# Differential values of both head pairs in one product with 512 moving columns, heads started one chunk earlier in the chunk list, background step every 16 matmuls

## The chip, the cores and the metric

The kernel runs on one core of a Trainium2 chip. The metric is the device time of one execution in microseconds (us), less is better. The engines named below are TensorE (PE, with its weight loads as PEld), VectorE (DVE), ScalarE (ACT), GpSimd (POOL) and SyncE (SP). "Product" means a matrix product of the kernel, made of many PE matmuls.

## The reference, cut to what matters

One layer over 512 prompt tokens and 64 sample tokens, model width 1024, all in float32: a half-step SwiGLU feed-forward, a mixer with one combined projection, and a second half-step SwiGLU feed-forward, each between two RMSNorms.

```
x = x + 0.5 * rms(swiglu(rms(x)))
h = rms(x);  p = h @ w_in          # columns: retention q|k|v|gate, differential q1q2|k1k2|v
q_d = rope(q_d.reshape(b, l, 4, 2, 64)); k_d = rope(...)
v_d = v_d.reshape(b, l, 4, 128)    # 4 heads of 128 columns; an output of its own (new_v)
a = softmax(s1) - lam * softmax(s2);  diff = rms(a @ v_d)
x = x + rms(concat(ret, diff) @ w_out)
x = x + 0.5 * rms(swiglu(rms(x)))
```

The changed product is `v_d`: 576 tokens x 1024 by 1024 x 512 columns, that is two pairs of heads with 256 columns each.

## The kernel before, in words

Tokens are cut into two halves of 256 and 320 (the second holds 256 prompt and 64 sample tokens). Every product is made with both operands split into a high and a low fp32r part (`whi`/`wlo` of a weight tile, `hhi`/`hlo` of the input), so each 128-deep step takes three matmuls. A weight tile is 128 x 512; SP loads it (256 KB, `raw`), ACT casts it to `whi` (L126) and DVE subtracts to `wlo` (L127). Twelve such pairs are held.

The mixer runs from 404.3 us to about 724 us of the span. Its projection is cut into 14 chunks of 256 columns in the order `IN_ORDER`: vd0, qd0, kd0, qd1, kd1, vd1, kr0, qr0, vr0, kr1, qr1, vr1, gr0, gr1 (d differential, r retention, 0 and 1 the head pair), then four chunks of the output projection. Each chunk is done for half 0 and then half 1. The first `FIRST` = 3 chunks form a group: all three for half 0, then all three for half 1, so that the boundary from the first feed-forward can finish half 1 meanwhile. In a q, k or gate chunk the weights are stationary and 256 or 320 token columns move (L434 to L436). In a v chunk (`natural()`, L806 to L808) 128 tokens are stationary and the chunk's 256 weight columns move, 48 matmuls a half; the 64 sample tokens of half 1 are a third block with 16 matmuls (`sample()`).

PSUM has two double buffers `pm` (a product's two banks) and four single banks `ps`. A q or k product in a `pm` buffer is read by three DVE instructions of `rotate()`: a shuffle (L757), and two multiplications (L758, L759). L757 and L758 read the PSUM buffer, so it is free when L758 is done. The next product but one needs that buffer.

Attention of a pair of heads is "background": `heads()` is a generator (score products `sc`, row maxima on DVE, exponentials on ACT, transposes `tp`, products with the values `av`, and for the differential pairs a final norm `finish()` with the sums `oss`). It is added to `self.bg` after a chunk given by `plan` (pair d0 after kd0, d1 after vd1, r0 after vr0, r1 after vr1). `pump()` counts the matmuls of the running product and makes one step of it for every `PUMP` = 18. Emission order is what the engines get, apart from the static order that the Tile scheduler derives from it. Before the first output chunk (`chunks[14]`) what is left in the background is drained.

Of the kernel before, what the change touches and what calls it, by code (L numbers as in the profile page):

```python
# [37 lines left out]
W_BUFS = 12  # L38
RK = 2
RAW_BUFS, RAW2_BUFS = 3, 5  # L40
FIRST, LAST_FFN, LAST_MIX = 3, 4, 3
PUMP = 18
B_NOW = {2: 2, 4: 0}
QK_BUFS = 5
WARM = 11
V_PS = (("vd", 0),)
N2 = 7


# [4 lines left out]
NB = (((0, 0, 128), (1, 128, 128)), ((2, 0, 128), (3, 128, 128), (4, 256, 64)))  # L54


class Weights:
# [6 lines left out]
        self.nc, self.raw, self.pool, self.raw2 = nc, raw_pool, w_pool, None  # L64
        self.parts, self.src, self.loaded, self.done = [], [], [], []

    def add(self, ap, nk, both=False):

        first = len(self.parts)
        for k in range(0, nk, RK):  # L70
            self.parts.append(("plain", len(self.src)))
            self.src.append((ap[:, k:k + RK, :], both and len(self.src) % 3 > 0))
        return list(range(first, len(self.parts)))

    def unit(self, ap):
# [72 lines left out]


class Layer:  # L150
    IN_ORDER = [("vd", 0), ("qd", 0), ("kd", 0), ("qd", 1), ("kd", 1), ("vd", 1), ("kr", 0), ("qr", 0), ("vr", 0),
                ("kr", 1), ("qr", 1), ("vr", 1), ("gr", 0), ("gr", 1)]

    def __init__(self, nc, tc, ctx, io):
# [573 lines left out]
    def mixer(self, h, post_g, next_g):  # L728
        nc, tc, io = self.nc, self.tc, self.io
# [5 lines left out]
        with ExitStack() as ctx:  # L735
            pool = lambda name, bufs=1: ctx.enter_context(tc.tile_pool(name=name, bufs=bufs))
            rt, qkp, vp, pp, atp, cp, op = (
                pool("rt"), pool("qk", QK_BUFS), pool("vp"), pool("pp", 3), pool("atp", 1), pool("cp"), pool("op"))
            rope = {}
            q, k, v, gate = {}, {}, {}, {}  # L740
# [21 lines left out]
            def project(name, c, half):  # L762
                n = HN[half]
                kind = name[-1]
                if name[0] == "v":
                    return natural(name, c, half)
                if name[0] in "qk" and (kind, half) not in rope:
                    tables(kind, half)
                ps = self.product(self.w_in[name, c], half, self.h_parts(h, half))[0][1]
                if name[0] == "g":  # L770
                    g = gf = qk_tile(half, "gate")
                    nc.vector.tensor_tensor(gf, ps, r[half].unsqueeze(1).broadcast_to([P, 2, n]), ALU.mult)
                    nc.scalar.activation(gf, gf, AF.Silu)
                    gate[c, half] = g
                    return
                a, b = rotate(ps, kind, half)
                t = qk_tile(half, name)
                nc.vector.tensor_tensor(t, a, b, ALU.add)
                for kk in range(2):
                    (q if name[0] == "q" else k)[kind, 2 * c + kk, half] = t[:, kk, :]  # L780
                if name == "kd":
                    nc.gpsimd.dma_start(out=io["k_out"][:, 2 * c:2 * c + 2, HOFF[half]:HOFF[half] + n], in_=t)

            def natural(name, c, half):

                kind = name[-1]
                pieces = self.w_in[name, c]
                hp = self.h_parts(h, half)
                for first in range(0, len(NB[half]), 2):
                    blocks = NB[half][first:first + 2]  # L790
                    if (name, c) in V_PS:
                        ps = self.ps1("psv").rearrange("p (b d) -> p b d", b=2)
                    else:
                        ps = self.pm.tile([P, 2, 512], F32, tag="pm", name="pmv")
# [17 lines left out]
                    t = vp.tile([P, 2, 256], F32, tag="v2", name=name, bufs=4)  # L812
                    for bi, (b, off, m) in enumerate(blocks):
                        nc.scalar.activation(t[:m, bi, :], ps[:m, bi, :256], AF.Copy,
                                             scale=self.rnat[half][:m, first + bi:first + bi + 1])
                        for kk in range(2):
                            v[kind, 2 * c + kk, b] = t[:m, bi, kk * P:(kk + 1) * P]
                        if name == "vd":
                            nc.gpsimd.dma_start(out=io["v_out"][b * P:b * P + m, c * 256:(c + 1) * 256],
                                                in_=t[:m, bi, :])  # L820

            def sample(name, c, pieces, ps):
# [12 lines left out]
                for kk in range(2):  # L835
                    v[name[-1], 2 * c + kk, 4] = t[:TS, kk * P:(kk + 1) * P]
                if name == "vd":
                    nc.gpsimd.dma_start(out=io["v_out"][TP:, c * 256:(c + 1) * 256], in_=t[:TS, :])

            def o_tiles(shared):  # L840
                if shared:
# [296 lines left out]
            def heads(kind, pair):  # L1138
                o = held[kind, pair] = o_tiles((kind, pair) == ("r", 0))
                make = diff_items if kind == "d" else ret_items  # L1140
                yield from pipeline(make(2 * pair, o) + make(2 * pair + 1, o))
                if kind == "d":
                    yield from finish(kind, pair)

            held = {}
            plan = {("kd", 0): [lambda: heads("d", 0)], ("vd", 1): [lambda: heads("d", 1)],
                    ("vr", 0): [lambda: heads("r", 0)], ("vr", 1): [lambda: heads("r", 1)]}

            def proj(name, c):
# [12 lines left out]
            chunks[14] = (chunks[14][0], lambda half, fn=chunks[14][1]: (self.drain(), fn(half)))  # L1162
            self.run(self.halves(chunks, FIRST, LAST_MIX))
        return after

    def build(self):
        nc, io = self.nc, self.io
        self.w_in = {}
        self.plan = [self.ffn_weights(0)]
        for i, key in enumerate(self.IN_ORDER):  # L1170
            self.w_in[key] = self.w.add(io["win"][i], KT)
# [30 lines left out]
        h = []  # L1202
# [14 lines left out]
        h = self.ffn(0, h, 0, 1, 2)  # L1217
# [82 lines left out]
def arrays_of(inp):  # L1300

    c = np.ascontiguousarray
    a = {}
# [19 lines left out]
    perm = ret_perm()  # L1323
    perm2 = np.concatenate([perm, 128 + perm])
    win = []
    for name, ch in Layer.IN_ORDER:
# [43 lines left out]
```

## Time and profile before

| what | value |
|---|---|
| median of 3 runs | 1130.77 us (1130.28 to 1130.91) |
| profiled execution | 1130.78 us, span 1129.0 us, 1.8 us lie around the span |
| PE busy over the span | 1115.6 us (99%) |
| DVE busy | 840.9 us (74%) |
| ACT busy | 579.5 us (51%) |
| POOL busy | 39.0 us (3%) |
| granted TensorE clock, mean | 0.996 |

The busy times overlap. A row of the timeline has a start, a duration, the engine, the line, what is written and read with shapes, a count where like instructions follow each other, and in brackets the idle time of that engine just before it and what ended it. Successive PE matmuls overlap, so a matmul costs the distance of two starts, not its duration.

### The profile page before, as it was taken

Reading aid. Unit: us, or ns where it says so; the run is one execution under the profiler, and the core shown is the slowest. Engines: PE = TensorE matmul, PEld = TensorE weight load, DVE = VectorE, ACT = ScalarE, POOL = GpSimd, SP = SyncE. Lnnn points to the kernel's source line nnn. Section 1 sums busy time; section 2 is a strip of 40 time slices with the busy share of each in tenths; the row PEclk is TensorE's granted clock in tenths of the full one; section 3 lists DMA queues with packets and bytes.
Section 4 is the critical chain, followed back from the end, with each engine's and each line's share of the span. In section 5 each row is a group of like instructions: output and inputs, shape, how many; then the busy total and the mean of one; then the engine's idle time right before and its main releaser. Section 6 shows DMA issues by size and latency. Waiting matters only on the chain.

```text
span 1129.0 us, 21258 instructions
## 1 busy us (share of the span) xinstructions
PE 1115.6 (99%) x8308; PEld 1096.2 (97%) x8308; DVE 840.9 (74%) x1646; ACT 579.5 (51%) x1112; POOL 39.0 (3%) x76
## 2 busy tenths in 40 slices
PE   8999999999999999999999999999999999999997
PEld 8999999999999999898999999999999999999997
DVE  7898865876587499869775585899886578658745
ACT  7666632562365465555442555666555156325543
POOL 0000000000000020010001010100000000000000
PEclk9999999999999999999999999999999999999999
DMA  8303431351236133332313221640334124313602
GB/s 278 90 29 113 125 101 38 106 139 55 76 88 212 39 115 106 97 110 60 98 58 89 83 69 39 198 120 16 92 115 135 38 85 124 101 38 105 203 2 84
DMA packets 57317, 109.22 MB, mean 97 GB/s; under 512 B 7008, under 2 KB 10336, under 8 KB 57216
## 3 DMA queue, kind: packets, MB, share of 16 engines
q1 hardware_dynamic: 51856, 91.97, 27.7%
q0 software_dynamic: 4352, 14.68, 3.9%
q8 instruction: 65, 1.06, 0.4%
q10 hardware_dynamic: 1008, 1.20, 0.3%
q14 instruction: 36, 0.29, 0.1%
HBM read 100.23 MB, written 7.60 MB: 96 GB/s over the span
## 4 chain that ended last, share of the span: by engine, by line
PE 90%; DVE 5%; DMA 2%; ACT 2%; issue 1%; DVEq 0%; SPq 0%; ACTq 0%
PE pm L435 11%; PE pm L434 11%; PE pm L436 11%; PE A L529 7%; PE A L530 7%; PE A L531 7%; PE C L531 3%; PE C L530 3%; PE C L529 3%; PE pb L434 2%; PE pa L434 2%; PE pb L436 2%; PE pa L435 2%; PE pa L436 2%; PE pb L435 2%; PE B L529 2%
## 5 line engine op out<-in xcount | busy, mean ns | idle before, releaser
L126 ACT CAST whi<-raw 128x512 fp32r<-128x512 f32 x336 | 206.7, 619 | 258.6 <-PE pm L435 98.4
L127 DVE TENSOR_TENSOR wlo<-raw,whi 128x512 fp32r<-128x512 f32 x336 | 229.6, 688 | 84.9 <-ACT whi L126 80.0
L434 PE MATMUL pm<-hhi,whi 128*128 128x320 f32 (+1 forms) x496 | 151.6, 306 | 1.9 <-ACT hhi L254 1.9
L435 PE MATMUL pm<-hlo,whi 128*128 128x320 f32 (+1 forms) x496 | 148.5, 299 | 0.3 <-DVE hlo L255 0.3
L436 PE MATMUL pm<-hhi,wlo 128*128 128x320 f32 (+1 forms) x496 | 148.1, 299 | 0.0
L434 PE MATMUL pm<-a,whi 128*128 128x320 f32 (+1 forms) x452 | 134.0, 297 | 0.4 <-ACT y L661 0.4
L435 PE MATMUL pm<-a,whi 128*128 128x320 f32 (+1 forms) x452 | 134.0, 297 | 0.4 <-DVE a L187 0.4
L436 PE MATMUL pm<-a,wlo 128*128 128x320 f32 (+1 forms) x452 | 134.1, 297 | 0.0
L529 PE MATMUL A<-tb,whi 128*128 128x288 f32 x432 | 128.0, 296 | 0.0
L530 PE MATMUL A<-tb,whi 128*128 128x288 f32 x432 | 127.5, 295 | 0.0
L531 PE MATMUL A<-tb,wlo 128*128 128x288 f32 x432 | 127.0, 294 | 0.0
L126 ACT CAST whi<-wsum 128x512 fp32r<-128x512 f32 x108 | 67.1, 621 | 68.8 <-PE A L530 17.0
L434 PEld LDWEIGHTS pm<-hhi,whi 128*128 128x128 f32 x496 | 94.8, 191 | 4.3 <-ACT hhi L254 2.1
L435 PEld LDWEIGHTS pm<-hlo,whi 128*128 128x128 f32 x496 | 94.8, 191 | 1.1 <-DVE hlo L255 0.5
L436 PEld LDWEIGHTS pm<-hhi,wlo 128*128 128x128 f32 x496 | 94.7, 191 | 0.1
L127 DVE TENSOR_TENSOR wlo<-wsum,whi 128x512 fp32r<-128x512 f32 x108 | 74.6, 691 | 21.2 <-ACT whi L126 18.9
L434 PEld LDWEIGHTS pm<-a,whi 128*128 128x128 f32 x452 | 85.8, 190 | 0.7 <-ACT y L661 0.6
L435 PEld LDWEIGHTS pm<-a,whi 128*128 128x128 f32 x452 | 85.8, 190 | 0.6 <-DVE a L187 0.6
L436 PEld LDWEIGHTS pm<-a,wlo 128*128 128x128 f32 x452 | 85.8, 190 | 0.0
L531 PEld LDWEIGHTS A<-tb,wlo 128*128 128x128 f32 x432 | 81.3, 188 | 0.0
L529 PEld LDWEIGHTS A<-tb,whi 128*128 128x128 f32 x432 | 80.9, 187 | 0.2
L530 PEld LDWEIGHTS A<-tb,whi 128*128 128x128 f32 x432 | 81.1, 188 | 0.0
(348 smaller groups left out, 2904.0 us busy)
## 6 DMA issues: line engine op xcount, KB each, us to landing
raw<-in_w0gs SPq DMA_DIRECT2D x72, 256.0 KB, 2.7
raw<-in_w1gs SPq DMA_DIRECT2D x72, 256.0 KB, 2.7
raw<-in_win SPq DMA_DIRECT2D x56, 256.0 KB, 3.1
raw<-in_w0d SPq DMA_DIRECT2D x44, 256.0 KB, 2.8
raw<-in_w1d SPq DMA_DIRECT2D x44, 256.0 KB, 2.8
raw<-in_w0gu SPq DMA_DIRECT2D x16, 256.0 KB, 5.8
raw<-in_wout SPq DMA_DIRECT2D x16, 256.0 KB, 3.0
raw<-in_w1gu SPq DMA_DIRECT2D x16, 256.0 KB, 3.4
```

What stands on the lines that cost most here:

```text
L126: nc.scalar.copy(hi, raw)
L127: nc.vector.tensor_tensor(lo, raw, hi.bitcast(F32), ALU.subtract)
L434: nc.tensor.matmul(outs[c], lhsT=hi[:, k, cs], rhs=rh, start=kt == 0, stop=False)
L435: nc.tensor.matmul(outs[c], lhsT=hi[:, k, cs], rhs=rl, start=False, stop=False)
L436: nc.tensor.matmul(outs[c], lhsT=lo[:, k, cs], rhs=rh, start=False, stop=kt == len(kts) - 1)
L529: nc.tensor.matmul(out, lhsT=hi[:, k, :], rhs=rh, start=first and k == 0, stop=False, skip_group_check=True)
L530: nc.tensor.matmul(out, lhsT=hi[:, k, :], rhs=rl, start=False, stop=False, skip_group_check=True)
L531: nc.tensor.matmul(out, lhsT=lo[:, k, :], rhs=rh, start=False, stop=last and k == 3, skip_group_check=True)
```

## The change

The two vd chunks become one, first in the list, with weights `wvd` whose 128 x 512 tiles each hold one 128-deep step of all 512 columns (`rk=1`) instead of two steps of 256. `wide()` makes the product with 512 moving columns into a `pm` buffer, one bank for each block of 128 tokens; `wide_sample()` does the sample tokens into one `ps` bank. The evictions then go to four tiles as before. There are 13 instead of 14 input chunks; the first group holds two chunks (`FIRST_MIX`); pair d1 is added to the background after kd1 where before it was after vd1; and `PUMP` is 16. Pair d0 is still added after kd0, which now is the third chunk run alone. The order `vd, qd0, kd0, qd1, kd1` puts four chunks' worth of products before kd0's end instead of three. Tiles of the values get a tag for each pair.

```diff
-FIRST, LAST_FFN, LAST_MIX = 3, 4, 3
-PUMP = 18
+FIRST, LAST_FFN, FIRST_MIX, LAST_MIX = 3, 4, 2, 3
+MIX_IN = 13
+PUMP = 16
-V_PS = (("vd", 0),)
...
-    IN_ORDER = [("vd", 0), ("qd", 0), ("kd", 0), ("qd", 1), ("kd", 1), ("vd", 1), ("kr", 0), ("qr", 0), ("vr", 0),
+    IN_ORDER = [("vd", 0), ("qd", 0), ("kd", 0), ("qd", 1), ("kd", 1), ("kr", 0), ("qr", 0), ("vr", 0),
...
+                if name == "vd":
+                    return wide(name, half)
...
+            def wide(name, half):
+                pieces = self.w_in[name, 0]
+                hp = self.h_parts(h, half)
+                for first in range(0, len(NB[half]), 2):
+                    blocks = NB[half][first:first + 2]
+                    if len(blocks) == 1:
+                        wide_sample(name, pieces)
+                        continue
+                    ps = self.pm.tile([P, 2, 512], F32, tag="pm", name="pmv")
+                    for bi, (b, off, m) in enumerate(blocks):
+                        for kt, i in enumerate(pieces):
+                            whi, wlo = self.w.done[i]
+                            rh, rl = (t[:, off:off + m] for t in hp(kt))
+                            o = ps[:m, bi, :]
+                            nc.tensor.matmul(o, lhsT=rh, rhs=whi, start=kt == 0, stop=False)
+                            nc.tensor.matmul(o, lhsT=rh, rhs=wlo, start=False, stop=False)
+                            nc.tensor.matmul(o, lhsT=rl, rhs=whi, start=False, stop=kt == KT - 1)
+                            self.pump(6)
+                    self.late_rms(half)
+                    for c in range(2):
+                        t = vp.tile([P, 2, 256], F32, tag=f"v2{c}", name=name, bufs=2)
+                        for bi, (b, off, m) in enumerate(blocks):
+                            nc.scalar.activation(t[:m, bi, :], ps[:m, bi, c * 256:(c + 1) * 256], AF.Copy,
+                                                 scale=self.rnat[half][:m, first + bi:first + bi + 1])
...
+            def wide_sample(name, pieces):
+                ps = self.ps1("psv")
...
-            plan = {("kd", 0): [lambda: heads("d", 0)], ("vd", 1): [lambda: heads("d", 1)],
+            plan = {("kd", 0): [lambda: heads("d", 0)], ("kd", 1): [lambda: heads("d", 1)],
...
-            self.run(self.halves(chunks, FIRST, LAST_MIX))
+            self.run(self.halves(chunks, FIRST_MIX, LAST_MIX))
...
+            self.w_in[key] = self.w.add(io["wvd"], KT, rk=1) if key[0] == "vd" else self.w.add(io["win"][i - 1], KT)
```

Four pieces of the engines' order show where the change moves work. Names carry the program's buffer numbers.

The first is PE before, at the place where the second half of the first group begins its values: `psv` is the value product of pair 0, `hhi`/`hlo` the split input, and the input numbers 4791, 4842 and 4895 are its second, third and fourth quarter.

```order
L806 MATMUL psv_5283<-whi_4619,hhi_4842 128x256
L807 MATMUL psv_5283<-wlo_4620,hhi_4842 128x256
L808 MATMUL psv_5283<-whi_4619,hlo_4843 128x256
L806 MATMUL psv_5283<-whi_4668,hhi_4895 128x256
L807 MATMUL psv_5283<-wlo_4669,hhi_4895 128x256
L808 MATMUL psv_5283<-whi_4668,hlo_4896 128x256
L806 MATMUL psv_5283<-whi_4668,hhi_4895 128x256
L807 MATMUL psv_5283<-wlo_4669,hhi_4895 128x256
L808 MATMUL psv_5283<-whi_4668,hlo_4896 128x256
```

The second is PE of the changed kernel at the start of the same product: `pm_5175` is qd0 of half 0, `pmv_5231` the value product of half 1.

```order
L434 MATMUL pm_5175<-hhi_4895,whi_5065 128x256
L435 MATMUL pm_5175<-hlo_4896,whi_5065 128x256
L436 MATMUL pm_5175<-hhi_4895,wlo_5066 128x256
L833 MATMUL pmv_5231<-whi_4607,hhi_4741 128x512
L834 MATMUL pmv_5231<-wlo_4608,hhi_4741 128x512
L835 MATMUL pmv_5231<-whi_4607,hlo_4742 128x512
L833 MATMUL pmv_5231<-whi_4613,hhi_4741 128x512
L834 MATMUL pmv_5231<-wlo_4614,hhi_4741 128x512
L835 MATMUL pmv_5231<-whi_4613,hlo_4742 128x512
```

Before, three chunks of half 0 (144 matmuls) stood ahead of half 1, and a quarter of the input served six matmuls of 256 columns; now vd and qd0 (96 matmuls) stand ahead of it, and six matmuls of 512 columns use a quarter.

The third is PE before where qr0 ends its half 0 (`pm_6661`) and begins half 1 (`pm_6784`), which takes the buffer that kr0 of half 1 (`pm_6482`) held.

```order
L434 MATMUL pm_6661<-hhi_4895,whi_6331 128x256
L435 MATMUL pm_6661<-hlo_4896,whi_6331 128x256
L436 MATMUL pm_6661<-hhi_4895,wlo_6332 128x256
L434 MATMUL pm_6784<-hhi_4741,whi_6116 128x320
L435 MATMUL pm_6784<-hlo_4742,whi_6116 128x320
L436 MATMUL pm_6784<-hhi_4741,wlo_6117 128x320
```

The fourth is PE of the changed kernel at that same place: `pm_6447` is qr0 of half 0, `pm_6602` qr0 of half 1, which takes the buffer that kr0 of half 1 (`pm_6277`) held; `sc`, `tp` and `av` belong to the attention of pair d1.

```order
L436 MATMUL pm_6447<-hhi_4895,wlo_6163 128x256
L987 MATMUL tp_6412<-cst_958,p_6327 128x128
L996 MATMUL av_6466<-at_6414,vd_5135 128x128
L966 MATMUL sc_6471<-kd_6035,qd_5858 128x256
L966 MATMUL sc_6471<-kd_6151,qd_5858 128x256
L966 MATMUL sc_6472<-kd_6035,qd_5858 128x256
L966 MATMUL sc_6472<-kd_6151,qd_5858 128x256
L987 MATMUL tp_6491<-cst_958,p_6366 128x128 x2
L434 MATMUL pm_6602<-hhi_4741,whi_5874 128x320
L435 MATMUL pm_6602<-hlo_4742,whi_5874 128x320
```

Before, the first matmuls of qr0 half 1 followed qr0 half 0 directly; now a transpose, a value product, four score matmuls and two more transposes of pair d1 stand ahead of them, and pair d1 is only at its fourth score tile (`sc_6471`).

The fifth and sixth are DVE of the changed kernel: first where `finish()` of pair d0 (`fsq`, `fo`) runs, with the rotation of kr0 half 0 (`pm_6181`) among it, ...

```order
L194 SCALAR_TENSOR_TENSOR fo_6243<-fo_6243,fy_6242 128x2x256
L187 TENSOR_TENSOR flo_6264<-fsq_6261,fhi_6263 128x640
L908 SCALAR_TENSOR_TENSOR fo_6243<-o_5594,dg_966,fo_6243 128x2x256
L757 STREAM_SHUFFLE rb_6268<-pm_6181 128x2x256
L758 TENSOR_TENSOR ra_6267<-pm_6181,rt_6178 128x2x256
L187 TENSOR_TENSOR mlo_6258<-fo_6243,mhi_6257 128x2x256
L759 TENSOR_TENSOR rb_6268<-rb_6268,rt_6178 128x2x256
L903 TENSOR_SCALAR fsq_6261<-oss_6298 128x320
L780 TENSOR_TENSOR kr_6272<-ra_6267,rb_6268 128x512
```

... and then, thirty rows later, where kr0 half 1 (`pm_6277`) is rotated, behind the scores of pair d1 (`p`, `rz`).

```order
L978 TENSOR_SCALAR p_6366<-p_6366,rz_6358 128x256
L971 TENSOR_SCALAR mx_6389<-mx_6389 128x1 x2
L979 SCALAR_TENSOR_TENSOR p_6366<-p_6371,rz_6358,p_6366 128x256
L757 STREAM_SHUFFLE rb_6417<-pm_6277 128x640
L758 TENSOR_TENSOR ra_6416<-pm_6277,rt_6274 128x640
L976 RECIPROCAL rz_6391<-zz_6390 128x2
L759 TENSOR_TENSOR rb_6417<-rb_6417,rt_6274 128x640
L977 TENSOR_TENSOR rz_6391<-rz_6391,neglam_976 128x1
L978 TENSOR_SCALAR p_6401<-p_6401,rz_6391 128x384
L780 TENSOR_TENSOR kr_6421<-ra_6416,rb_6417 128x640
```

Before, 79 DVE instructions stood from the first `fsq` of that `finish()` to the L758 of kr0 half 1, which frees its buffer; now 49 stand there, because pair d1 has come less far: two of its score tiles, the scores of the sample tokens and two weight tiles come later.

## Rows read from the trace of the kernel before

**Rows 1.** The page's first part: span, then busy time of each engine.

```profile
span 1129.0 us, 21258 instructions
...
PE 1115.6 (99%) x8308; PEld 1096.2 (97%) x8308; DVE 840.9 (74%) x1646; ACT 579.5 (51%) x1112; POOL 39.0 (3%) x76
```

**Rows 2.** Waits of PE in the mixer, 404 to 725 us: total, times, longest.

```profile
PE ssq_post L224 <- DVE sq_post L221: 1.0, 1, 1.0
PE psv L806 <- ACT hhi L254: 0.6, 1, 0.6
PE ssq_pre L224 <- DVE sq_pre L221: 0.6, 1, 0.6
```

**Rows 3.** Busy time of the engines in four stretches of the mixer.

```profile
core 0: us, PE busy (x) PEld busy (x) DVE busy (x) ACT busy (x) POOL busy (x), PEclk, DMA share, GB/s
411.90:425.80 13.90, 13.85 (x111) 13.64 (x112) 13.77 (x29) 6.96 (x18) 3.10 (x6) 1.00 0.32 97
500.00:510.00 10.00, 10.00 (x85) 10.00 (x84) 4.41 (x8) 6.50 (x12) 2.17 (x4) 1.00 0.21 68
520.00:530.00 10.00, 10.00 (x67) 8.56 (x64) 9.39 (x35) 5.51 (x16) 0.57 (x1) 1.00 0.11 27
503.77:533.73 29.96, 29.88 (x216) 26.91 (x215) 26.62 (x83) 18.23 (x45) 2.19 (x4) 1.00 0.21 60
```

**Rows 4.** PE matmul groups of the value products, 404 to 760 us, shapes apart.

```profile
L806 PE MATMUL pmv<-whi,hhi 128*128 128x256 f32 x96 | 28.0, 291 | 0.0
...
L806 PE MATMUL psv<-whi,hhi 128*128 128x256 f32 x32 | 9.4, 293 | 0.6 <-ACT hhi L254 0.6
```

**Rows 5.** PE timeline: matmuls of 256 moving columns back to back.

```profile
414.18 0.28 PE L806 MATMUL psv<-whi,hhi 128*128 128x256 f32 x1
414.30 0.28 PE L807 MATMUL psv<-wlo,hhi 128*128 128x256 f32 x1
```

**Rows 6.** PE timeline: sample scores of 512 columns, then 320 columns.

```profile
463.45 1.02 PE L972 MATMUL scs<-kc,lq 128*128 128x512 f32 x2
464.31 0.33 PE L972 MATMUL scs<-kd,lq 128*128 128x64 f32 x2
464.48 0.50 PE L945 MATMUL tp<-cst,p 128*128 128x128 f32 x3
464.73 0.39 PE L434 MATMUL pm<-hhi,whi 128*128 128x320 f32 x1
464.95 0.30 PE L435 MATMUL pm<-hlo,whi 128*128 128x320 f32 x1
465.10 0.31 PE L436 MATMUL pm<-hhi,wlo 128*128 128x320 f32 x1
```

**Rows 7.** PE timeline: the value product of half 1 at its fourth input quarter.

```profile
425.82 0.28 PE L808 MATMUL psv<-whi,hlo 128*128 128x256 f32 x1
426.71 0.38 PE L806 MATMUL psv<-whi,hhi 128*128 128x256 f32 x1 [0.61 <-ACT hhi L254]
426.93 0.28 PE L807 MATMUL psv<-wlo,hhi 128*128 128x256 f32 x1
427.30 0.39 PE L808 MATMUL psv<-whi,hlo 128*128 128x256 f32 x1
427.52 0.28 PE L806 MATMUL psv<-whi,hhi 128*128 128x256 f32 x1
427.64 0.28 PE L807 MATMUL psv<-wlo,hhi 128*128 128x256 f32 x1
427.76 0.39 PE L808 MATMUL psv<-whi,hlo 128*128 128x256 f32 x1
427.98 0.28 PE L806 MATMUL psv<-whi,hhi 128*128 128x256 f32 x1
```

**Rows 8.** DVE timeline at the same place.

```profile
426.69 1.01 DVE L255 SCALAR_TENSOR_TENSOR hlo<-x,gain,hhi 128x320 fp32r<-128x320 f32 x2
```

**Rows 9.** DVE timeline: start of d0's finish, two score rows, kr0 half 1 rotated.

```profile
503.77 0.76 DVE L861 TENSOR_SCALAR fsq<-oss 128x256 f32<-128x256 f32 x2 [4.70 <-PE oss L860]
...
525.31 0.68 DVE L928 TENSOR_REDUCE mx<-sc 128x1 f32<-128x512 f32 x1
525.91 0.61 DVE L937 SCALAR_TENSOR_TENSOR p<-p,rz 128x384 f32<-128x384 f32 x1
...
532.92 0.81 DVE L758 TENSOR_TENSOR ra<-pm,rt 128x640 f32<-128x640 f32 x1
```

**Rows 10.** PE timeline: qr0 half 1 begins; scores alone and in a row.

```profile
534.39 0.70 PE L924 MATMUL sc<-kd,qd 64*128 64x256 f32 x2
...
543.89 0.31 PE L434 MATMUL pm<-hhi,whi 128*128 128x320 f32 x1
...
545.08 1.13 PE L924 MATMUL sc<-kd,qd 64*128 64x256 f32 x8
```

More of the change, by code (lines that the diff above doesn't have):

```diff
@@ L65, in __init__, with add @@
         self.parts, self.src, self.loaded, self.done = [], [], [], []
-    def add(self, ap, nk, both=False):
+    def add(self, ap, nk, both=False, rk=RK):
         first = len(self.parts)
-        for k in range(0, nk, RK):
+        for k in range(0, nk, rk):
             self.parts.append(("plain", len(self.src)))
-            self.src.append((ap[:, k:k + RK, :], both and len(self.src) % 3 > 0))
+            self.src.append((ap[:, k:k + rk, :], both and len(self.src) % 3 > 0))
         return list(range(first, len(self.parts)))
@@ L790, in natural @@
                     blocks = NB[half][first:first + 2]
[L791 to L794, printed above, removed]
+                    ps = self.pm.tile([P, 2, 512], F32, tag="pm", name="pmv")
                     if len(blocks) == 1:
@@ L811, in natural @@
                     self.late_rms(half)
-                    t = vp.tile([P, 2, 256], F32, tag="v2", name=name, bufs=4)
+                    t = vp.tile([P, 2, 256], F32, tag=f"v2{c}", name=name, bufs=2)
                     for bi, (b, off, m) in enumerate(blocks):
@@ L817, in natural @@
                             v[kind, 2 * c + kk, b] = t[:m, bi, kk * P:(kk + 1) * P]
-                        if name == "vd":
+            def wide(name, half):
[6 more added lines that the diff above has]
+                        continue
+                    ps = self.pm.tile([P, 2, 512], F32, tag="pm", name="pmv")
+                    for bi, (b, off, m) in enumerate(blocks):
[9 more added lines that the diff above has]
+                    for c in range(2):
+                        t = vp.tile([P, 2, 256], F32, tag=f"v2{c}", name=name, bufs=2)
+                        for bi, (b, off, m) in enumerate(blocks):
+                            nc.scalar.activation(t[:m, bi, :], ps[:m, bi, c * 256:(c + 1) * 256], AF.Copy,
+                                                 scale=self.rnat[half][:m, first + bi:first + bi + 1])
+                            for kk in range(2):
+                                v["d", 2 * c + kk, b] = t[:m, bi, kk * P:(kk + 1) * P]
@@ L819, in natural @@
                             nc.gpsimd.dma_start(out=io["v_out"][b * P:b * P + m, c * 256:(c + 1) * 256],
                                                 in_=t[:m, bi, :])
+            def wide_sample(name, pieces):
+                ps = self.ps1("psv")
+                for kt, i in enumerate(pieces):
+                    for part in range(2):
+                        nc.tensor.matmul(ps, lhsT=self.hs[kt // 4][:, kt % 4].rearrange("p s t -> p (s t)"),
+                                         rhs=self.w.done[i][part], start=kt == 0 and part == 0,
+                                         stop=kt == KT - 1 and part == 1)
+                    self.pump(4)
+                for c in range(2):
+                    cs = slice(c * 256, (c + 1) * 256)
+                    t = vp.tile([P, 256], F32, tag="v1", name=name, bufs=2)
+                    nc.scalar.copy(t[:TS, :], ps[TS:P, cs])
+                    nc.vector.tensor_tensor(t[:TS, :], ps[:TS, cs], t[:TS, :], ALU.add)
+                    nc.scalar.activation(t[:TS, :], t[:TS, :], AF.Copy, scale=self.rnat[1][:TS, 2:3])
+                    for kk in range(2):
+                        v["d", 2 * c + kk, 4] = t[:TS, kk * P:(kk + 1) * P]
+                    nc.gpsimd.dma_start(out=io["v_out"][TP:, cs], in_=t[:TS, :])
@@ L836, in sample @@
                     v[name[-1], 2 * c + kk, 4] = t[:TS, kk * P:(kk + 1) * P]
-                if name == "vd":
-                    nc.gpsimd.dma_start(out=io["v_out"][TP:, c * 256:(c + 1) * 256], in_=t[:TS, :])
             def o_tiles(shared):
@@ L1161, in mixer @@
             chunks += [(self.w_out[j], out_proj(j)) for j in range(4)]
-            chunks[14] = (chunks[14][0], lambda half, fn=chunks[14][1]: (self.drain(), fn(half)))
-            self.run(self.halves(chunks, FIRST, LAST_MIX))
+            chunks[MIX_IN] = (chunks[MIX_IN][0], lambda half, fn=chunks[MIX_IN][1]: (self.drain(), fn(half)))
+            self.run(self.halves(chunks, FIRST_MIX, LAST_MIX))
         return after
@@ L1170, in build @@
         for i, key in enumerate(self.IN_ORDER):
-            self.w_in[key] = self.w.add(io["win"][i], KT)
+            self.w_in[key] = self.w.add(io["wvd"], KT, rk=1) if key[0] == "vd" else self.w.add(io["win"][i - 1], KT)
         self.w_out = [self.w.add(io["wout"][j], KT) for j in range(4)]
@@ L1325, in arrays_of @@
     win = []
-    for name, ch in Layer.IN_ORDER:
+    a["wvd"] = c(cols(w[:, off["vd"]:], 512)[0])
+    for name, ch in Layer.IN_ORDER[1:]:
         blk = w[:, off[name] + 256 * ch:off[name] + 256 * ch + 256]
```

## The prediction, made before the changed kernel was timed

> **What bounds the kernel now.** I read the page's totals first: PE is busy 1115.6 of 1129.0 us, 99%, and no other engine comes near [rows 1]. That share hides where time can still be won, so I went to the stretch that the change touches, the mixer, and asked for PE's waits there: three of any size, together 2.2 us in 320 us [rows 2]. So almost everything on the path is PE's own issue time, and the change can win by issuing less or by removing one of those waits. It can lose by making PE wait where it does not wait now. The table of stretches says where that is likely: at the start of the mixer DVE is busy 13.77 of 13.90 us, in the attention of the differential pairs 9.39 of 10, with one loose stretch (4.41 of 10) between the two pairs [rows 3]. The reader is to see there that PE is the bound with a second engine close behind it. Moving background work against PE's products therefore matters more than the DVE total of 74% suggests.
>
> **Issue of the value product.** Two pairs, per pair 48 matmuls for half 0, 48 for half 1 and 16 for the sample tokens: 224 matmuls of 256 moving columns before, 112 of 512 after. The groups show 283 to 293 ns for one [rows 4], but matmuls overlap, and the timeline has starts 0.12 us apart at 256 columns [rows 5] and 0.147 (464.95 to 465.10 is 0.15, with two digits) at 320 [rows 6]. 256 columns at 2.4 GHz are 106.7 ns, 320 are 133.3, so both carry 13.3 ns beyond the columns. The granted clock is 1.00 in these stretches [rows 3]. 224 x 0.120 = 26.9 us before. After, my estimate is 512 / 2.4 + 13.3 = 226.7 ns, 112 x 0.2267 = 25.4 us: **-1.5 us**. Bounds: the trace has no split matmul of 512 columns. The nearest rows are the sample scores, two instructions of 512 columns from 463.45 to 464.31, 0.43 us each, that is 0.215 for each of the two passes that plain float32 takes [rows 6]; at 0.215 the saving is 26.9 - 24.1 = 2.8 us. At 0.240 (nothing gained by halving the count) it is 0. I take 226.7 because the fp32r rows at 256 and 320 share the 13.3 ns, and the score rows are another type.
>
> The Trainium skill, "TensorE: Matmul & The Clock Gate", section "Back-to-back issue gap", gives two figures for 512 columns: about 216 ns for an isolated gap, and about 131 ns per matmul sustained with weight loads in the stream. By the first the saving would be 2.7 us. By the second it would be an estimated 12.2 us; the trace's 0.215 per pass [rows 6] speaks against it.
>
> **The start of the mixer.** Value product of half 1: the fourth quarter of its input is late. From 425.82 to 427.98 PE makes seven steps; at 0.12 they take 0.84 us, the rows take 2.16, so **1.3 us** are lost [rows 7]. Half of it is the visible wait for `hhi`, the rest for `hlo`, which DVE makes from 426.69 to 427.7 [rows 8], behind a full queue. After the change this product starts when vd and qd0 of half 0 are through instead of vd0, qd0 and kd0: 48 x 0.2267 + 48 x 0.12 = 16.6 us instead of 144 x 0.12 = 17.3, so 0.6 us earlier. Before, the fourth quarter is reached 18 matmuls in (2.2 us); after, also 18 in, but 18 x 0.2267 = 4.1 us. The need thus moves from 425.9 to about 425.9 - 0.6 + 1.9 = 427.2 us, and `hlo` only 0.45 us later as the third matmul. `hhi` is there at 426.7 and `hlo` by 427.2 for the first of the quarter's two blocks. I take the whole 1.3 us as gone, **-1.3 us**; if DVE reaches `hlo` 0.5 us later than now, 0.8 remain won. The two waits for `ssq_pre` and `ssq_post` [rows 2] I leave: `ssq_pre` of half 0 still comes about 7 us into the mixer (31 x 0.2267 = 7.0, before 58 x 0.12 = 7.0), and `ssq_post` belongs to the boundary with the second feed-forward.
>
> **Edits at nothing.** The weight tiles are the same eight of 256 KB for vd, cast by the same instructions; the evictions have the same sizes, now all from ACT early, where ACT is half idle (6.96 of 13.90 us) [rows 3]. The value outputs go out earlier on POOL's queue, where nobody waits for them. If that cover were gone, an eviction delayed past the second next product in `pm` would show as a wait of PE.
>
> **The background step at 16.** A chunk has 48 matmuls, so 18 gave a step at 18, 36, 54, and now three steps in each. The count of places where PE goes back from attention matmuls to a product rises from 85 to 88 over the mixer by the engines' order. Going back costs 0.22 instead of 0.147 us for the first matmul [rows 6], and about as much again on entry is possible: 3 x 0.1 = **+0.3 us**, bounds 0 and 0.6.
>
> **The seam between the two differential pairs.** Before, vd1 (112 matmuls, 13.4 us) stands between kd1 and kr0 and needs no DVE but one small add. `finish()` of d0 falls into it, and DVE idles 4.70 us before its first `fsq` [rows 9]; this is the loose stretch of 4.41 in 10 us [rows 3]. After the change vd1's time is gone from here. Pair d1's scores, `finish()` of d0 and the two rotations of kr0 now meet. What is late next is the `pm` buffer that kr0 half 1 holds: qr0 half 1 wants it and DVE must first do its L758.
>
> Before, DVE reaches the end of that L758 29.96 us after the first `fsq` (503.77 to 533.73), 26.62 of them busy [rows 3, 9], and PE wants the buffer at 543.89 [rows 10]: slack 10.2 us. After, 30 of those 79 DVE instructions stand behind the rotation. Their starts in the trace, from one to the next, add up to 7.3 us (for example 0.60 for the reduction at 525.31, then 0.5 for the row after it) [rows 9]. So DVE needs 26.6 - 7.3 = 19.3 us from the first `fsq` without a pause.
>
> PE in that time has 48 matmuls of kr0 half 1 at 0.147 (7.0 us), 48 of qr0 half 0 at 0.12 (5.8), four `oss` at 0.147 (0.6), twelve score matmuls between 0.14 each in a row of eight and 0.35 in a pair [rows 10], say 0.22, 2.6 us, four transposes and value products at 0.12 (0.5), and six returns at 0.1 (0.6): 17.1 us. DVE is **2.2 us late, +2.2 us**. Bounds: PE's 17.1 is uncertain by 1 us either way, and DVE's 19.3 can grow by up to 1.5 us, if half of the 3.3 idle us in the old stretch were waits for ACT that come again. That gives 1.2 to 4.7 us; below that a gain of the earlier pm release at kr0 half 0 could bring it to 0.5.
>
> **The sum.** -1.5 - 1.3 + 0.3 + 2.2 = -0.3 us on the profiled execution's 1130.78 us (span 1129.0 and 1.8 around it), which is the median of the runs to 0.01: **1130.5 us**. A measurement of this kernel tells a change from none at about 0.2%, 2.26 us, so that is "the same".
>
> **Rivals.**
> - **A, no wait at the seam.** DVE keeps up, because its 19.3 us shrink or PE's order holds more work than I priced. Then 1130.78 - 1.5 - 1.3 + 0.3 = 1128.3 us, faster by just over the bound; with the issue at 0.215 us it is 1127.0. For it: in the old stretch DVE ran with slack of 10 us. Against: that slack came from 13.4 us of vd1 and from score tiles that no longer stand there. It decides in favour of "faster" when the seam costs under 0.2 us, or under 1.5 us at 0.215 a matmul.
> - **B, a larger wait at the seam: slower.** One mechanism: DVE's instructions at the seam stand in fixed order behind exponentials of ACT for three score tiles, and ACT is itself at 18.23 of 29.96 us [rows 3]. If each costs 1.3 us more, the wait is 2.2 + 3.9 = 6.1 us and the time 1134.4. It decides for "slower" from 4.8 us of waiting.
> - **C, the wide product saves nothing** (0.240 us a matmul): 1132.0 us. Against: the common 13.3 ns in two shapes.
> - **D, wide matmuls overlap each other beyond their columns.** If one cost no more than the 0.147 us of a 320-column row, 112 x 0.147 = 16.5 us would be left of 26.9, and the time 1130.5 + 1.5 - 10.4 = 1121.6 us. Against: 0.215 us a pass in the row that has 512 columns, and 512 columns alone are 213 ns at the granted clock. The Trainium skill's "TensorE: Matmul & The Clock Gate" ("Back-to-back issue gap") is what speaks for it.
>
> **How the numbers follow.** Chances: forecast (seam 1 to 4.7 us) 0.44, A 0.31, B 0.19, C 0.04, D 0.02. The forecast and C lie within 0.2%, but 0.03 of the forecast, where the issue gains 2.8 us, is on the fast side, as A and D are; B is slower: faster 0.36, same 0.45, slower 0.19. The range leaves out D, the far end of A and most of B: 1126.9 to 1133.8 us. For the likeliest case alone it is 1128.5 to 1133.
>
> **What would show it.** The value matmuls start 0.227 us apart (0.215 for the bound, 0.24 for C). PE has no wait for `hhi` in the first group's half 1. A wait of PE appears for DVE's L758 at the first matmuls of qr0 half 1, with DVE busy without a break from `fsq` to there. If PE shows no such wait, A is right; if DVE shows idle time behind ACT's exponentials in that stretch and PE waits over 4.8 us, B is. Wrong altogether would be a new wait elsewhere, above all at the `pm` buffers of the first group, where the value product of half 0 now holds one until its inverse RMS is known.

## The result and the profile after

The changed kernel takes 1138.22 us (median of 4 runs, 1137.44 to 1140.33) against 1130.53 us for the kernel before in the same comparison: ratio 1.0073, 95% interval 1.0061 to 1.0084. It is slower by 7.7 us. The profiled execution took 1137.44 us with a span of 1135.6 us, 6.7 us more than the profiled execution before.

The first part of its page, to be held against [rows 1]:

```profile
span 1135.6 us, 21034 instructions
...
PE 1119.2 (99%) x8196; PEld 1091.4 (96%) x8196; DVE 840.2 (74%) x1646; ACT 577.7 (51%) x1112; POOL 38.8 (3%) x76
```

112 matmuls fewer, DVE and ACT busy as before: nobody has more instructions to do, and still PE's busy time grows by 3.6 us and the span by 6.6. PE's waits in the mixer, 404 to 728 us (total, times, longest), to be held against [rows 2]:

```profile
PE oss L901 <- ACT fhi L186: 1.3, 1, 1.3
PE av L996 <- ACT at L989: 1.0, 3, 0.5
PE tp L987 <- DVE sc L969: 0.8, 1, 0.8
PE cent L1100 <- ACT raw L186: 0.4, 1, 0.4
PE tp L987 <- DVE mx L971: 0.4, 1, 0.4
PE pm L434 <- DVE gate L774: 0.3, 1, 0.3
```

The two waits at the mixer's start (`psv` for `hhi`, `ssq_pre`) are gone, and new ones stand nearly all ahead of attention matmuls (`oss`, `av`, `tp`, `cent`). They add up to 4.2 us, so they are not the whole loss either. The third row of [rows 2], `ssq_post`, belongs to the boundary behind the mixer, at 731.45 us here and so outside this list; it went from 1.0 to 1.5 us.

The first group went as forecast, and a little better. PE timeline of the wide product, then of half 1 where its fourth input quarter begins (it answers to [rows 5] and [rows 7]):

```profile
407.00 0.39 PE L834 MATMUL pmv<-wlo,hhi 128*128 128x512 f32 x1
407.22 0.39 PE L835 MATMUL pmv<-whi,hlo 128*128 128x512 f32 x1
407.45 0.39 PE L833 MATMUL pmv<-whi,hhi 128*128 128x512 f32 x1
...
426.12 0.39 PE L835 MATMUL pmv<-whi,hlo 128*128 128x512 f32 x1
426.35 0.39 PE L833 MATMUL pmv<-whi,hhi 128*128 128x512 f32 x1
426.57 0.39 PE L834 MATMUL pmv<-wlo,hhi 128*128 128x512 f32 x1
426.80 0.39 PE L835 MATMUL pmv<-whi,hlo 128*128 128x512 f32 x1
```

Starts are 0.227 us apart (0.45 for two), and there is no gap where `hhi` and `hlo` were late. From the mixer's first matmul to the end of the first group it takes 41.1 us (404.02 to 445.14). Before, 44.0 us (404.28 to 448.24) held kd0 (12.8 us by issue) and lacked vd1 (13.4), which makes 44.6 for the same work: 3.5 us won. The input's fourth quarter also came sooner than in the kernel before. ACT's instructions that make its `hhi`, before and then in the changed kernel:

```profile
426.09 1.01 ACT L254 ACTIVATE hhi<-x,gain 128x320 fp32r<-128x320 f32 x2 [0.44 <-DVE x L315]
...
425.22 1.02 ACT L254 ACTIVATE hhi<-x,gain 128x320 fp32r<-128x320 f32 x2 [0.44 <-DVE x L315]
```

So the loss lies behind the first group. To find it I cut the rest of the mixer at four places that both kernels have (first score of pair d0, first `oss` of d0's finish, first retention score, first product of the gated output; the last stretch, "out", ends where the second feed-forward begins), and took from each stretch's length what its product matmuls need at the prices of 0.120, 0.147 and 0.227 us a start. What is left, the attention's own matmuls and every wait or slow start of PE, is a number that can be compared although products were moved:

| us beside product issue | d0 | d1 | retention | out | sum |
|---|---|---|---|---|---|
| before | 21.5 | 25.8 | 20.8 | 9.4 | 77.5 |
| changed | 22.9 | 30.8 | 22.9 | 10.8 | 87.4 |

9.9 us more, of which 5.0 are in the stretch of pair d1. There the scores take 9.3 us instead of 7.6 (starts to next starts) and PE stands idle 1.5 us instead of 0.1; about 1.9 of the 5.0 us are neither. The place where I expected the wait shows how. PE and then DVE of the changed kernel:

```profile
522.82 0.70 PE L966 MATMUL sc<-kd,qd 64*128 64x256 f32 x2
...
524.23 0.70 PE L966 MATMUL sc<-kd,qd 64*128 64x256 f32 x2
...
530.01 0.30 PE L987 MATMUL tp<-cst,p 128*128 128x128 f32 x1 [0.37 <-DVE mx L971]
...
530.79 0.49 PE L996 MATMUL av<-at,vd 128*128 128x128 f32 x2 [0.48 <-ACT at L989]
531.21 2.30 PE L966 MATMUL sc<-kd,qd 64*128 64x256 f32 x8
533.44 0.44 PE L987 MATMUL tp<-cst,p 128*128 128x128 f32 x2
533.64 0.41 PE L434 MATMUL pm<-hhi,whi 128*128 128x320 f32 x1
```

```profile
512.71 0.76 DVE L903 TENSOR_SCALAR fsq<-oss 128x256 f32<-128x256 f32 x2 [2.30 <-PE oss L902]
514.16 0.69 DVE L192 TENSOR_TENSOR fo<-fy 128x512 f32<-128x512 f32 x1 [0.70 <-ACT fy L904]
...
532.77 0.81 DVE L758 TENSOR_TENSOR ra<-pm,rt 128x640 f32<-128x640 f32 x1
```

DVE needs 20.9 us from `fsq` to the end of L758 (forecast 19.3), and qr0 half 1 begins at 533.64, as soon as the buffer is free. But PE does not stand waiting for the buffer: it is late already, since the transpose, the value product and the scores of d1 that stand ahead are late one after the other, 0.37 and 0.48 us idle, and eight score entries take 2.30 us where eight took 1.13 before [rows 10]. DVE is nearly full at this place: of its 20.9 us it pauses 1.7, nearly all of them before 517 us.

The second thing to see is the rows of `x2`. A score matmul has 64 contraction rows and is made in two passes: it has two entries, `x2`, in the timeline, where the order in front of the prediction has one row. In the kernel before, the matmuls of the two components mostly stand together (60 of 96 score entries start within 0.015 us of another, 40 of 96 in the changed kernel):

```profile
451.80 0.70 PE L924 MATMUL sc<-kd,qd 64*128 64x256 f32 x4
```

Two matmuls in 0.70 us there, one in 0.70 us here (0.63 us to the next start in both cases): two score matmuls side by side cost what one does. The changed order puts them apart at several places, and score entries take 16.1 us in all where they took 14.0 before (starts to next starts).

### The profile page after: what moved, and what is told of

It is laid out like the page before. It is cut to its first block, busy times and chain, and to the rows that moved or that the text cites. A ratio compares the mean times of both kernels' runs of the same rounds, so it can differ in the third digit from the quotient of the medians.

```text
span 1135.6 us, 21034 instructions
## 1 busy us (share of the span) xinstructions
PE 1119.2 (99%) x8196; PEld 1091.4 (96%) x8196; DVE 840.2 (74%) x1646; ACT 577.7 (51%) x1112; POOL 38.8 (3%) x76
## 4 chain that ended last, share of the span: by engine, by line
PE 87%; DVE 6%; DMA 3%; ACT 2%; issue 1%; SPq 0%; DVEq 0%; ACTq 0%
PE pm L434 10%; PE pm L435 10%; PE pm L436 10%; PE A L529 7%; PE A L530 7%; PE A L531 7%; PE C L531 3%; PE C L530 3%; PE C L529 3%; PE pb L434 2%; PE pa L434 2%; PE pb L436 2%; PE pa L435 2%; PE pa L436 2%; PE pb L435 2%; PE B L529 2%
```

## The experiments

Each is compared with the kernel before on its own chip; medians of the kernel before there lie between 1130.2 and 1130.8 us. The changed kernel stands at ratio 1.0073.

**The step.** The changed kernel with `PUMP = 18`, and the kernel before with 16:

```diff
-PUMP = 16
+PUMP = 18
```

> The changed kernel with one background step per 18 matmuls, as before. Theory P (steps every 16 reach the attention matmuls before DVE and ACT have made their inputs, and that is the loss): 1127 to 1130 us, and the waits of PE for background inputs (tp, av, oss; 4.5 us in the changed kernel) fall under 1.5. Theory S (the missing cover between pair d0 and pair d1 is the loss, whatever the step): 1136 to 1139 us. Theory T (retention part loses 4 us to the step, differential part 6 to the cover): about 1134.

Measured: 1137.07 us, ratio 1.0062 (1.0050 to 1.0075).

> The kernel before with one background step per 16 matmuls and nothing else. Theory P: 1134 to 1139 us, PE waiting for tp, av and oss. Theory S: within 1 us of 1130.5. Theory T: about 1134, the loss after the last differential pair.

Measured: 1133.82 us, ratio 1.0032 (1.0020 to 1.0045). PE's waits in its mixer, the longest three:

```profile
PE oss L859 <- ACT fhi L186: 1.3, 1, 1.3
PE psv L806 <- ACT hhi L254: 0.7, 1, 0.7
PE cent L1058 <- ACT raw L186: 0.4, 1, 0.4
```

So the step of 16 costs the kernel before 3.7 us, and the waits that come with it (`oss` 1.3, `cent` 0.4) are ones that the changed kernel shows too. But giving the changed kernel its 18 back wins only 1.2 us, which the noise of the two medians can make. The waits for `tp`, `av` and `oss` did fall under 1.5 us as theory P asked, from 3.5 in the list above (not 4.5) to 1.0, and the time did not follow. Neither P nor S holds alone, and the two do not add. With 18 the stretches of d0 and d1 get longer (24.4 and 31.3 us beside product issue), the retention shorter (17.9), and what is left over lands at the end (13.2 instead of 10.8). Scores then take 20.6 us. The changed kernel with 18 is also where the forecast wait shows, at the first matmul of qr0 half 1:

```profile
534.51 0.38 PE L434 MATMUL pm<-hhi,whi 128*128 128x320 f32 x1 [1.03 <-DVE ra L758]
```

One reason why the two do not add is in the list of chunks. After pair d0 is added, the kernel before has 1104 matmuls of input chunks to spread the attention over, 61 steps of 18. The changed order has vd1's 112 fewer, 992: 55 steps of 18 or 62 of 16. Of the 189 (before 187) matmul entries of the retention attention 54 fell behind the first product of the gated output before, 51 in the changed kernel, 76 in it with 18.

**The place of pair d1.** Added after kr0, with a step of 16 and of 18:

```diff
-("kd", 1): [lambda: heads("d", 1)],
+("kr", 0): [lambda: heads("d", 1)],
```

> The changed kernel with pair d1 added to the background after kr0, one chunk later, so that a chunk of 92 matmuls stands between as vd1 did before. Theory S: 1128 to 1132 us. Theory P: 1136 to 1139 us, since the step is still 16. Theory T: about 1132.

Measured: 1134.94 us, ratio 1.0040 (1.0028 to 1.0053), between all three ranges.

> Both: pair d1 added after kr0 and a step per 18. Both theories expect what the wide product alone brings: 1127 to 1128.5 us (1.5 us of issue, 1.3 of the wait at the mixer's start). If it stays at 1133 or above, neither the step nor the place of d1 is the cause, and the order of the first group or pair d0's later start is.

Measured: 1135.46 us, ratio 1.0048 (1.0034 to 1.0061). Starting d1 a chunk later gives back 3.3 us of the 7.7 with the step of 16. A chunk of rotated products in between is not the cover that vd1 was. By what was expected of it, 1133 or more says that the cause lies in neither the step nor d1's place but in the first group's order or pair d0's later start. No run changes these two alone; the version below that reaches 1129.91 us keeps both as they are in the changed kernel, so they do not by themselves cost the 7.7 us. With 18 PE waits for L758 at qr0 half 1 here too, 1.5 us.

**The width alone.** The wide product issued as two of 256 columns (the same for the sample tokens), everything else as changed:

```diff
-                            o = ps[:m, bi, :]
+                        for cs in (slice(0, 256), slice(256, 512)):
+                            ...
+                                o = ps[:m, bi, cs]
```

> The changed kernel with each 512-column value matmul split into two of 256, everything else as changed. By the row spacing (0.227 us against two of 0.120): 224 x 0.120 - 112 x 0.227 = 1.5 us more in the first group, and the same total on top of the changed kernel, 1139.5 us. If the width changes nothing: 1138.2.

Measured: 1141.64 us, ratio 1.0095 (1.0081 to 1.0108), 3.4 us above the changed kernel and not 1.5. The split is not width alone: its loop goes through all eight steps of the input for the first 256 columns and then again for the other 256, so it needs the late quarter after half as much PE time. In its first group the trace has 43.9 us instead of 41.1, and PE's waits have the one for `hhi` again:

```profile
PE pmv L834 <- ACT hhi L254: 0.6, 1, 0.6
```

So of the 2.8 us in the first group 1.5 are issue and about as much is the wait for the input, which half 1 reaches too early again. The last 0.6 us are within what this order varies by: its profiled execution also has 25.8 us instead of 22.9 in the stretch of d0, where the program is the same.

**An extra product as cover.** A product that the kernel does not need, where vd1 stood:

```diff
+            chunks.insert(5, (self.w_in["kr", 0], cover))
-("kd", 1): [lambda: heads("d", 1)],
```

> The changed kernel with a step per 18 and with an extra product of 112 matmuls of 256 columns (kr0's weights, result not used) between kd1 and kr0, where vd1 stood before; pair d1 is added after it. The extra product is work that the kernel does not need, 13.4 us of PE. Theory S (attention ran hidden under vd1, and lost that cover): all other losses vanish, so 1130.2 + 41.1 (vd and qd0 of the changed first group) + 12.8 (kd0) - 44.0 (first group before) = 1140 us. Rival O (the losses come from the new order of attention matmuls and steps as such, wherever products stand): e1's 1137.1 + 13.4 = 1150.5 us.

Measured: 1145.29 us, ratio 1.0129 (1.0115 to 1.0143). Halfway between the two: of the 13.4 us that the product costs, 5.2 come back against the changed kernel with a step of 18. They come back where the cover was missing: with its own issue taken off, the stretch of d1 is down to 25.0 us (31.3 without it, 25.8 before the change).

**A value product that is needed, as cover.** vr0 goes ahead of kr0:

```diff
-("qd", 1), ("kd", 1), ("kr", 0), ("qr", 0), ("vr", 0),
+("qd", 1), ("kd", 1), ("vr", 0), ("kr", 0), ("qr", 0),
...
-("kd", 1): [lambda: heads("d", 1)],
-("vr", 0): [lambda: heads("r", 0)]
+("vr", 0): [lambda: heads("d", 1)],
+("qr", 0): [lambda: heads("r", 0)]
```

> The changed kernel with vr0 moved ahead of kr0, so that a value product, which needs no DVE, stands where vd1 stood; pair d1 is added after it, pair r0 after qr0, a step per 18. Nothing is left out. Theory S with the loss local to the place between d0 and d1: 1127 to 1129 us, faster than before. Theory S with the loss in the total (one chunk of products less for the whole background): 1132 to 1135 us. Rival O: 1135 or more.

Measured: 1134.86 us, ratio 1.0036 (1.0022 to 1.0050). That is inside the range for a loss in the total and at the edge of rival O's, so this run does not tell them apart.

> The same with a step per 16. If the 3.7 us that the step of 16 cost in the kernel before come here too, 3 to 4 us above the one with 18. If the step of 16 makes up for the lost chunk (background ends in time), below it: 1127 to 1130 us.

Measured: 1129.91 us, ratio 0.9998 (0.9990 to 1.0007), 8.3 us faster than the changed kernel. Here the step of 16 is the better one by 5 us, and of the two expectations the one holds in which the step makes up for the lost chunk. By place, the 5 us are in d0 and d1 (52.8 us together with 18, 47.7 with 16), and the scores alone make 4.3 of them (18.0 and 13.7 us). Why 18 sets the scores apart in this order no run shows. PE's waits in its mixer, and DVE around d0's finish:

```profile
PE ssq_post L224 <- DVE sq_post L221: 1.3, 1, 1.3
PE oss L901 <- ACT fhi L186: 1.3, 1, 1.3
PE tp L987 <- DVE sc L969: 0.8, 1, 0.8
```

```profile
511.99 0.76 DVE L903 TENSOR_SCALAR fsq<-oss 128x256 f32<-128x256 f32 x2 [2.59 <-PE oss L902]
514.58 0.69 DVE L192 TENSOR_TENSOR fo<-fy 128x512 f32<-128x512 f32 x1 [1.83 <-ACT fy L904]
```

The waits for `av`, `cent` and `gate` are gone, DVE has more idle time in d0's finish (1.83 us behind the first `fsq`, in the changed kernel 0.70), and the stretch of d1 costs 24.9 us beside product issue instead of 30.8, less than before the change. Scores take 13.7 us.

A denser step still, 15:

> The kernel with vr0 ahead of kr0 and a step per 15 instead of 16 (18, 30 and 48 in a product of 48). If the background wants to end earlier: 1128 to 1129.5. If denser steps cost waits as the step of 16 did in the kernel before: 1131 to 1134.

Measured: 1130.99 us, ratio 1.0004 (0.9995 to 1.0014), about 1 us above 16 and not clear of it by the intervals. It falls between the two ranges and decides nothing.

**Is it DVE?** Rotations of kr0 and qr0 reduced, in the changed kernel and in the one before:

```diff
+                if kind == "r" and c == 0:
+                    nc.vector.tensor_tensor(t, ps, rope[kind, half][:, 0:1, :].broadcast_to([P, 2, n]), ALU.mult)
+                else:
                     a, b = rotate(ps, kind, half)
```

> The changed kernel with the rotations of kr0 and qr0 cut to one DVE multiplication of four instructions (the sine part is left out, so q and k of the first retention pair are not rotated): 2.1 us less of DVE for half 0 and 2.5 us for half 1, four times, 9 us between pair d0 and pair d1. Theory V (DVE is late there, as predicted): 5 to 7 us of the loss come back, 1131 to 1133. Theory K (what is lost is the order of the score matmuls and PE waits on banks and ACT): 1136 to 1138.

Measured: 1135.67 us, ratio 1.0045 (1.0033 to 1.0058).

> The control: the kernel before with the same cut, the same part left out. PE does not wait for DVE at this place in the kernel before, so both theories expect 1129.5 to 1131, no change; the part by which it is faster is to be taken off what the cut gives back in the changed kernel.

Measured: 1128.84 us, ratio 0.9982 (0.9974 to 0.9991). The cut gives the changed kernel 2.5 us and the control 1.9, where none was expected; of these 1.9 the control's scores make 1.0 (13.0 us instead of 14.0). In the stretch of d1 it is 2.4 against 1.6. By the medians 0.7 us belong to DVE's amount of work at this place, by the ratios 1.1. Each interval reaches about 1 us and more either way, so that is not clear of nothing, and it is not 5 to 7: with the step of 16 theory V falls. With 18, where PE does wait for L758, the cut was not run.

**Are the separated scores the cause?** Score matmuls of a query block kept together by order:

```diff
+                                if kh or c:
+                                    tc.keep_in_program_order(mm)
+                                self.pin = mm
...
+                    with self.behind():
                         nc.tensor.matmul(outs[c], lhsT=hi[:, k, cs], rhs=rh, start=kt == 0, stop=False)
```

> The changed kernel with the score matmuls of a query block held together in PE's order, by order constraints alone, with the next product matmul behind them. Theory K1 (the separation itself costs: two score matmuls of 64 rows run side by side when adjacent, 7 ns apart): scores fall from 16.1 us to 13.5 and the time to about 1135.5. Theory K2 (the second score matmul was put later because its PSUM bank was not free): PE waits at the scores instead, and the time stays at 1137 to 1140.

Measured: 1139.40 us, ratio 1.0076 (1.0063 to 1.0088). PE's waits from 500 to 590 us:

```profile
PE sc L972 <- DVE fsq L909: 1.1, 2, 0.8
PE oss L907 <- ACT fhi L186: 1.1, 1, 1.1
PE tp L996 <- DVE mx L980: 0.6, 1, 0.6
PE av L1005 <- ACT at L998: 0.6, 1, 0.6
PE sc L972 <- ACT ps L1031: 0.6, 1, 0.6
PE sc L972 <- ACT p L982: 0.5, 1, 0.5
```

K2: the scores now wait, for the readers of whatever tile last held their PSUM bank (`fsq` reads `oss`, `p` and `ps` are exponentials of earlier scores). So the order alone does not bring the scores side by side: 38 of 96 entries start within 0.015 us of another, and scores take 17.3 us. By this the separation was a symptom: the second score's bank was late, and the score was put where it could go. What scores that do run side by side would win in the changed kernel this run can't say.

**Early start or kind of product?** The version with vr0 ahead of kr0, but d1 added after kd1 as in the changed kernel:

```diff
-("vr", 0): [lambda: heads("d", 1)],
+("kd", 1): [lambda: heads("d", 1)],
```

> The kernel with vr0 ahead of kr0 and a step per 16, but pair d1 added after kd1 as in the changed kernel, so that vr0 runs under d1's own start and not ahead of it. Theory L (d1 starts too early: its steps follow those of d0 without a chunk between, and each step's inputs are late): back to 1135 to 1138. Theory M (it is the kind of product at this place: rotations of kr0 and its two PSUM buffers against a value product that DVE does not touch): 1130 to 1132, as with d1 later.

Measured: 1136.92 us, ratio 1.0055 (1.0041 to 1.0068). Theory L: with the early start nearly all of the loss is back, 7.0 us by the medians. The two profiled executions are 9.1 us apart, of which 3.4 are in the stretch of d1 and 5.9 in the retention's. Its trace shows a wait of the kind that was predicted, but at another place, the first matmul of kr1 half 1, which takes the buffer of qr0 half 1:

```profile
583.43 0.38 PE L434 MATMUL pm<-hhi,whi 128*128 128x320 f32 x1 [1.92 <-DVE ra L758]
```

Together with the kr0 version (1134.94) this says that both are needed: a later start of d1 over rotated products brings 3.3 us, a value product under an early start 1.3 (within the noise), a value product ahead of a later start 8.3.

**The step at the end.** The same version as the 1129.91 us, with a step of 18 from vr1 on:

```diff
+                    if half == 1 and (name, c) == ("vr", 1):
+                        self.every = 18
```

> The kernel with vr0 ahead of kr0, a step per 16 up to vr1 and per 18 from there on. If the step of 16 costs 2 us at the mixer's end (60.6 us from the first gated product to the second feed-forward before, 62.9 with it), 1127.5 to 1128.5 us and no wait of oss for fhi, faster than both kernels. If those 2 us come from the shifted phase of the steps and not from their number, 1129 to 1132.

Measured: 1128.37 us, ratio 0.9981 (0.9973 to 0.9990): the only complete kernel here that is faster than both. The time is in the range that was given, and the wait of `oss` for `fhi` is gone as expected. Its profile is of an execution of 1131.68 us, where the retention stretch is 19.2 us beside product issue (20.7 with 16) and the end 11.6 (11.7). So in that execution the gain is in the retention and not at the end, where it was expected; where it lies in the faster ones is open.

## Why the prediction was wrong, point by point

The forecast was 1130.5 us, the same; it came out at 1138.2, slower and above the range.

- **Issue of the value product (-1.5):** right. Starts are 0.227 us apart, so C and D fall. The bound of 0.215 rested on a misreading: the `x2` in [rows 6] is one score matmul in its two entries, so a pass of 512 columns took 0.43 us there, and no row shows 0.215 for 512 columns.
- **The start of the mixer (-1.3):** right, and a little more. The first group is 3.5 us shorter for the same work; besides the wait for the fourth quarter, the 0.6 us wait at `ssq_pre`, which I left in place, is gone as well [rows 2]. That the whole 1.3 came is in part luck: PE wanted the fourth quarter at 426.35 us and not at 427.2, ahead of the 426.7 at which I had `hhi` ready; but `hhi` itself came 0.87 us earlier.
- **The background step at 16 (+0.3):** this step failed. I counted returns of PE from attention to products and nothing else. Alone it costs 3.7 us in the kernel before: 1.4 in the last stretch, 1.9 in the retention, 0.9 in d0 (10.8, 22.6 and 22.4 us beside product issue), less 0.5 in d1. The changed kernel loses nearly the same there (1.3, 2.1 and 1.4). With three steps in every 48 matmuls, instead of two or three, attention matmuls come to PE before ACT and DVE have their inputs: `oss` waits 1.3 us for `fhi`, `cent` 0.4. These two are 1.7 of the 3.7 us; for the rest this cause is argued and not shown.
- **The seam (+2.2):** this step failed too. The place was right, and between 528 and 534 us PE loses about 2.4 us (by the distances of starts 0.5 at `tp`, 0.7 at `av`, 1.2 at the scores), but that this is close to 2.2 is luck. PE's 17.1 us counts twelve score matmuls at 0.22, which is the price of one entry in [rows 10], and each has two entries: by the same rows it is 5.3 us instead of 2.6, PE needs 19.7, and DVE with 19.3 would not be late. In the changed kernel these scores took 4.8 us; DVE took 20.9, that is its 19.3 and the pauses, and PE came to qr0 half 1 just as the buffer was free. So the forecast sign (a wait for L758 at qr0 half 1) did not show with the step of 16; it did in the two versions with 18 and vr0 in its old place (1.0 and 1.5 us). The term also was that of one buffer, while the stretch of d1 loses 5.0 us. What I gave as its cause, DVE's amount of work, came to 0.7 us by the medians of the cut and 1.1 by its ratios, neither clear of the noise. Nearly all of the loss hangs on the early start of pair d1 without a value product ahead of it.
- **Rival B** had the sign and asked for 4.8 us of waiting in one place by one mechanism, ACT's exponentials. The waits for ACT that the trace shows in pair d1 (`at`, 1.0 us in three, 0.5 of them ahead of qr0 half 1) are small, so B was not right either.

The sum of the changed kernel's profile is then -3.5 in the first group, +9.9 behind it (d0 +1.4, d1 +5.0, retention +2.1, end +1.3; the rounded parts give 9.8), and +0.3 from there on.

What stays open is which resource makes d1 late after an early start. Shown is that, with the step of 16, it is not DVE's total, that ordering the scores does not mend it, and that it is not the wait for one `pm` buffer. The chain from score over maximum, exponential, normalising and transpose to value product, with four single PSUM banks that d1's scores share with d0's `oss`, is what the waits in the version with paired scores point to; no run changed the number of banks.

## What to carry to other kernels

Work moved out of a hidden stretch takes its cover along: before moving a product that only one engine touches, ask which chains ran under it, and put another such product in its place; here that took the 7.7 us of loss away, and about 2 us were gained with a second step size. How often background work is interleaved must be priced by whether its inputs are ready and by how many matmuls are left to spread it over, not by its own issue time, and it has to be set again when the order changes: 16 was worse by 3.7 us in one order, better by 5 in another. To compare kernels whose order differs, take from each stretch what its main matmuls need at their issue price, and compare the rest. And when a row's price is multiplied by a count, make sure that both count the same thing: here the count was of matmuls and the price of entries.

## What the runs showed of the hardware that was not expected

- Two float32 score matmuls of 64 contraction rows that stand next to each other and use different rows cost together what one costs alone: 0.70 us in both rows above, `x4` (451.80) and `x2` (522.82), and 0.63 us to the next start in both.
- With fp32r the distance of starts was 0.120, 0.147 and 0.227 us at 256, 320 and 512 moving columns, the columns at 2.4 GHz plus 13 ns each, with one weight load to a matmul; the 13 ns were not smaller at the longer matmul. The Trainium skill's "TensorE: Matmul & The Clock Gate" gives 131 ns sustained at 512 columns ("Back-to-back issue gap"); this trace does not agree, it has 227.
